# Moving the row-major loads of a decoder trunk and padding a small tile ahead of its MLP's activations

## The chip, the core and the metric

The kernel runs on one core of a Trainium2 chip. The metric is device time of one execution in microseconds (us). PE is TensorE (the page lists its weight loads as PEld), DVE is VectorE, ACT is ScalarE, POOL is GpSimd; SP issues most of the DMAs.

## What is computed

Two decoder layers on 256 tokens of width 2048, all in float32. Each layer is a token mixer, a cross-attention to 256 memory rows and a squared-ReLU MLP of width 8192, each behind an RMSNorm, with plain residual adds, and a final RMSNorm.

```python
for i in range(2):
    h = rms_norm(x, g_mix[i])
    x = x + (chunked_gmlp(h, ...) if i == 0 else s5_glu(h, ...))
    x = x + memory_attention(rms_norm(x, g_xattn[i]), rms_norm(mem, g_mem[i]), ...)
    x = x + square(relu(rms_norm(x, g_ff[i]) @ w_up[i])) @ w_down[i]
return rms_norm(x, g_final)
```

The gMLP computes z = gelu(h @ w_in + b_in), a LayerNorm on one half of z, a 128x128 causal mix within each of 16 heads, a product with the other half, and an output projection.

## The kernel before

**Numbers in two parts.** Every float32 operand is split into a rounded high part and a low part (`split`, L100: an ACT copy makes the high part, a DVE subtraction the low part), and a product is three matmuls: high by high, high by low, low by high. Weights come from HBM in tiles of 512 KB (`wload`, L115, on SP's queue, four `wraw` buffers) and are split into `whi` and `wlo` (three buffers each). One weight tile feeds 12 matmuls of 512 columns in the token form (`gemm_tok`, L129; `gemm_hid`, L547), where the activation is the stationary operand and the weight the moving one. In the feature form (`gemm_feat`, L151) the weight is stationary; a pair is one matmul of 512 columns (L163) and one of 256 (L165).

**Order.** The Tile framework orders each engine's instructions at compile time, from priorities in program order and its own model of when inputs are ready; each engine then runs its list strictly in order. After each weight tile `tick` (L81) runs what is due: `at(n, f)` puts f behind n more ticks, and `side` is a list of which one entry is taken per tick. `lag` lowers the priority of what `side` runs.

**The start (gmlp, L275).** `features(j)` loads a feature-major chunk of x on SP's queue and scales it into the stationary operand. `tokens(j)` loads a row-major chunk of x (512 KB, SP's queue) and has ACT sum its squares (two `junk` squares, L176). `zin(n)` multiplies by one 512-column chunk of w_in (eight weight tiles, chunks 4 to 7 first) and evicts: rstd from the sums of squares, a bias load on POOL's queue, two DVE operations (L316), and a Gelu on ACT. During the first chunk `side` holds features 1 to 3 and tokens 0 to 3; then `flush` empties it. PSUM has two `acc` buffers, so chunk n+2 needs chunk n's eviction. `mixing(q)` prepares the spatial weights (a load, a POOL mask, a split); its `wsr` tile shares two buffers with the bias tiles. `mem_stats` (L246) loads the row-major memory rows in four chunks on POOL's queue into two buffers, for sums of squares that end in a small matmul (L258); it is written behind the first output chunk, but the loads need no input and the framework puts them early.

**The MLP (mlp, L510).** Four blocks per layer: eight `gemm_feat` make 16 hidden feature groups into tiles `hh` and `hl` (four each, 4096 bytes per partition), then four `gemm_hid` (L558 to L560) multiply them, as the stationary operand, by w_down. The last of layer 1 is `gemm_last` (L579 to L581). The pool `ml` begins with `r2`, two floats, before `hh`, `hl` and `r`; a tile takes a multiple of 32 bytes. In the program built from this kernel the addresses within a partition are, modulo 512 bytes:

| tiles | stationary | moving | matmuls |
|---|---|---|---|
| token form: `act` by `whi`, `wlo` | 448 | 448 | L145 to L147 |
| feature form: `whi`, `wlo` by `act` | 448 | 448 | L163, L165 |
| MLP layer 0: `hh`, `hl` by `whi`, `wlo` | 256 | 448 | L558 to L560 |
| MLP layer 1: `hh`, `hl` by `whi`, `wlo` | 352 | 448 | L558 to L560 |

All slices of these tiles start at multiples of 512 bytes from the tile's address.

Of the kernel before, what the change touches and what calls it, by code (L numbers as in the profile page):

```python
# [9 lines left out]
F32 = mybir.dt.float32  # L10
# [6 lines left out]
P = 128  # L17
# [4 lines left out]
NCH = D // NB  # L22
# [16 lines left out]
class Trunk:  # L39
# [75 lines left out]
    def wload(self, w, n, kc):  # L115
        raw = self.wp.tile([P, KB * NB], F32, name="wraw", bufs=4)
        k, c = w.shape[3:]
        self.nc.sync.dma_start(out=raw.rearrange("p (k c) -> p k c", k=k), in_=w[n, kc])
        return raw

    def wtile(self, w, n, kc, raw=None):
# [124 lines left out]
    def mem_stats(self, pool):  # L246

        nc = self.nc
        ss = self.new_ss()
        for j in range(NCH):  # L250
            m = pool.tile([P, 2, NB], F32, name="memc")
            nc.gpsimd.dma_start(out=m, in_=self.a["mem"][j])
            self.sumsq(m, ss, j)
        self.rstd_mem = self.rstd(ss, "rstd_mem", self.const)
        self.rows_mem = self.const.tile([P, 2, P], F32, name="rows_mem")
        pt = self.ps([P, 2, P])
        for t in range(2):
            nc.tensor.matmul(pt[:, t, :], self.rstd_mem[:, t:t + 1].broadcast_to([P, P]), self.ident,  # L258
                             start=(t == 0), stop=True, skip_group_check=True)
        nc.scalar.copy(out=self.rows_mem, in_=pt)  # L260
# [14 lines left out]
    def gmlp(self, x, nxt):  # L275
        nc, a, tc = self.nc, self.a, self.tc
        with tc.tile_pool(name="gm", bufs=2, reuse_waits="tile") as gp:
# [3 lines left out]
            def features(j):  # L281
                xt = gp.tile([P, 4, S], F32, name="memc")
                for h in range(0, 4, 2):
                    nc.sync.dma_start(out=xt[:, h:h + 2], in_=a["x_t"][j][:, h:h + 2])
                    if j == 0 and h == 0:
                        first.append(self.wload(a["a_w_in"], NCH, 0))
                self.scale_chunk(xt, 0, hT, j)

            def tokens(j):
                cs = slice(j * NB, (j + 1) * NB)  # L290
                nc.sync.dma_start(out=x[:, :, cs], in_=a["x"][j])
                self.sumsq(x[:, :, cs], ss, j)

            first = []
            features(0)
            self.lag = 0
            self.side += [lambda j=j: features(j) for j in range(1, NCH)]
            self.side += [lambda j=j: tokens(j) for j in range(NCH)]
            rstd = None

            vh = gp.tile([P, KT, 2, P], F32R, name="vh", bufs=1)
# [5 lines left out]
            def zin(n, out):  # L307
                nonlocal rstd
                acc = self.gemm_tok(hT, a["a_w_in"], n, raw=first)
                if rstd is None:  # L310
                    self.flush()
                    self.lag = 100
                    rstd = self.rstd(ss, "rstd")
                b = self.bc(gp, a["a_b_in"][n * NB:(n + 1) * NB])
                for t in range(2):
                    nc.vector.scalar_tensor_tensor(out=out[:, t, :], in0=acc[:, t, :], scalar=rstd[:, t:t + 1],  # L316
                                                   in1=b, op0=ALU.mult, op1=ALU.add)
                nc.scalar.activation(out=out, in_=out, func=AF.Gelu)

            def mixing(q):  # L320
                if q == 0:
                    nc.gpsimd.dma_start(out=bs, in_=a["b_s"])
                wr = gp.tile([P, 4, P], F32, name="wsr", tag="bc", bufs=2)
                nc.gpsimd.dma_start(out=wr, in_=a["w_s"][:, 4 * q:4 * q + 4, :])
                nc.gpsimd.affine_select(out=wr, in_=wr, pattern=[[0, 4], [1, P]], compare_op=ALU.is_ge,
                                        fill=0.0, base=0, channel_multiplier=-1)
                self.split(wsh[:, 4 * q:4 * q + 4, :], wsl[:, 4 * q:4 * q + 4, :], wr)

            v = self.act.tile([P, 2, NCH, NB], F32, name="v", tag="act")
            st = gp.tile([P, 2, NCH, 6], F32, name="st", bufs=1)  # L330
            for j in range(NCH):
                vc = v[:, :, j, :]
                zin(NCH + j, vc)
                if j == 1:
                    self.side += [lambda q=q: mixing(q) for q in range(4)]
                for t in range(2):
                    nc.vector.bn_stats(out=st[:, t, j, :], in_=vc[:, t, :])
            mv = gp.tile([P, 2, 2], F32, name="mv", bufs=1)
            for t in range(2):
                nc.vector.bn_aggr(out=mv[:, t, :], in_=st[:, t].rearrange("p a b -> p (a b)"))  # L340
# [49 lines left out]
            for j in range(NCH):  # L390
                if j == 3:
                    self.every = 1
                zin(j, us[j])
                if j:
                    self.at(1, lambda j=j: gate(j - 1, us[j - 1]))
                    self.at(3, lambda j=j: turn(j - 1, us[j - 1]))
# [6 lines left out]
            for j in range(NCH):  # L403
                if j == 0:
                    acc = self.gemm_tok(usT, a["a_w_out"], 0, acc=acc0, kts=range(12, KT), first=False)
                    self.mem_stats(gp)
                else:
                    acc = self.gemm_tok(usT, a["a_w_out"], j)
# [101 lines left out]
    def mlp(self, x, layer, cur, nxt):  # L510
        nc, a, tc = self.nc, self.a, self.tc
        wu, wd = a["f_w_up"][layer], a["f_w_down"][layer]
        hT = cur.act
        with tc.tile_pool(name="ml", bufs=4, reuse_waits="tile") as mp:
            r2 = mp.tile([P, 2], F32, name="r2", bufs=1)
            for b in range(DFF // D):
                hid = []
                for n in range(NCH):
                    h = mp.tile([P, 4, S], F32R, name="hh")
                    l = mp.tile([P, 4, S], F32R, name="hl")  # L520
                    for i in range(2):
                        r = mp.tile([P, 2, S], F32, name="r", bufs=2)
                        self.gemm_feat(hT, wu, 2 * (NCH * b + n) + i, r)
                        nc.vector.scalar_tensor_tensor(out=r, in0=r, scalar=0.0, in1=r, op0=ALU.max, op1=ALU.mult)  # L524
                        self.split(h[:, 2 * i:2 * i + 2], l[:, 2 * i:2 * i + 2], r)
                    hid.append((h, l))
                if b == 0:
                    rstd = cur.rstd()
                    nc.vector.tensor_tensor(out=r2, in0=rstd, in1=rstd, op=ALU.mult)
                if b == DFF // D - 1:  # L530
                    nxt.start()
                for n in range(NCH):
                    if nxt.closing and b == DFF // D - 1 and n == NCH - 1:
                        self.gemm_last(hid, wd, n, b * KT, lambda t, acc: (
                            nc.vector.scalar_tensor_tensor(  # L535
                                out=x[:, t, n * NB:], in0=acc, scalar=r2[:, t:t + 1],
                                in1=x[:, t, n * NB:], op0=ALU.mult, op1=ALU.add), nxt.finish(x, t)))
                        break
                    acc = self.gemm_hid(hid, wd, n, b * KT)
                    for t in range(2):  # L540
                        xc = x[:, t, n * NB:(n + 1) * NB]
                        nc.vector.scalar_tensor_tensor(out=xc, in0=acc[:, t, :], scalar=r2[:, t:t + 1], in1=xc,  # L542
                                                       op0=ALU.mult, op1=ALU.add)
                    if b == DFF // D - 1:
                        self.at(1, lambda n=n: nxt.chunk(x, n))
# [647 lines left out]
```

## Time and profile before

| | us |
|---|---|
| three runs: median (lowest, highest) | 2884.1 (2883.07, 2889.95) |
| the profiled execution: own time | 2886.18 |
| its span in the trace | 2884.4 |
| PE busy in the span | 2837.0 |
| DVE, ACT busy | 1831.7, 1332.5 |

The span is the time from the first to the last instruction that the profiler recorded; some 1.8 us of the execution lie outside it. Matmuls overlap, so PE counts as busy whenever one is in flight; how fast they follow each other is seen in their start times. A few per cent of matmul records can be missing.

### The profile page before, as it was taken

The numbers are of one execution on the slowest core, as the hardware profiler recorded it, in microseconds if no ns is written. First come the engines' busy times: TensorE is split into PE (matmuls) and PEld (weight loads), VectorE is DVE, ScalarE is ACT, GpSimd is POOL, SyncE is SP. The second block draws the span as 40 slices with busy tenths as digits, with TensorE's granted clock in tenths as the row PEclk, the third lists the DMA queues.
The fourth block names the chain that finished last, engine by engine and source line by source line (L and its number), as shares of the span: only waits on it lengthen the run. The fifth ranks groups of instructions, "written<-read, shape, count | busy, mean of one in ns | idle before, by whom it ended". The sixth has DMA issues, their size and how long they took to land.

```text
span 2884.4 us, 39580 instructions
## 1 busy us (share of the span) xinstructions
PE 2837.0 (98%) x15238; PEld 2365.6 (82%) x15238; DVE 1831.7 (64%) x2548; ACT 1332.5 (46%) x1714; POOL 205.4 (7%) x384
## 2 busy tenths in 40 slices
PE   8999999999999999999989999999999999999998
PEld 6778888888878888788867788888888888888886
DVE  5665655575778878787567566555556555465555
ACT  5445544444534444444455445444454344343443
POOL 1000000000022222222011000000000000000000
PEclk9999999999999999999999999999999999999999
DMA  8656655558677777777689766655566566666665
GB/s 276 216 187 192 195 176 175 176 175 232 193 215 212 224 218 222 214 219 207 214 243 281 224 201 210 184 175 183 173 185 190 188 186 188 187 192 185 188 188 148
DMA packets 180461, 579.55 MB, mean 201 GB/s; under 512 B 37440, under 2 KB 39664, under 8 KB 179504
## 3 DMA queue, kind: packets, MB, share of 16 engines
q1 hardware_dynamic: 140864, 509.67, 57.3%
q0 software_dynamic: 39264, 67.29, 8.6%
q8 instruction: 119, 1.95, 0.3%
q14 instruction: 70, 0.57, 0.1%
q10 hardware_dynamic: 144, 0.07, 0.0%
HBM read 553.88 MB, written 22.94 MB: 200 GB/s over the span
## 4 chain that ended last, share of the span: by engine, by line
PE 90%; DMA 4%; DVE 3%; issue 2%; ACT 1%; POOL 0%; SPq 0%; DVEq 0%; ACTq 0%; POOLq 0%
PE acc L163 24%; PE acc L165 12%; PE acc L560 8%; PE acc L559 8%; PE acc L558 8%; PE acc L146 8%; PE acc L147 8%; PE acc L145 8%; DVE wlo L102 1%; DMA wraw<-in_b_w_in 1%; PE ps L494 1%; PE ps L438 1%; PE ps L214 1%; DMA memc<-in_mem 1%; DMA wraw<-in_f_w_up 0%
## 5 line engine op out<-in xcount | busy, mean ns | idle before, releaser
L102 DVE TENSOR_TENSOR wlo<-wraw,whi 128x1024 fp32r<-128x1024 f32 x952 | 1164.4, 1224 | 859.6 <-ACT whi L101 857.2
L101 ACT CAST whi<-wraw 128x1024 fp32r<-128x1024 f32 x952 | 999.5, 1051 | 1314.1 <-PE acc L163 394.0
L163 PE MATMUL acc<-act,whi 128*128 128x512 f32 x3072 | 1080.4, 395 | 0.6 <-ACT whi L101 0.6
L165 PE MATMUL acc<-act,wlo 128*128 128x256 f32 x3072 | 866.1, 282 | 1.7 <-DVE wlo L102 1.6
L163 PEld LDWEIGHTS acc<-act,whi 128*128 128x128 f32 x3072 | 576.1, 188 | 130.6 <-issue 1.6
L165 PEld LDWEIGHTS acc<-act,wlo 128*128 128x128 f32 x3072 | 581.5, 189 | 6.6 <-DVE wlo L102 2.9
L145 PE MATMUL acc<-whi,act 128*128 128x512 f32 x1248 | 493.8, 396 | 13.2 <-ACT whi L101 11.8
L146 PE MATMUL acc<-wlo,act 128*128 128x512 f32 x1248 | 493.1, 395 | 10.5 <-DVE wlo L102 10.4
L147 PE MATMUL acc<-whi,act 128*128 128x512 f32 x1248 | 490.8, 393 | 0.3 <-DVE act L102 0.3
L560 PE MATMUL acc<-whi,hl 128*128 128x512 f32 x992 | 395.3, 399 | 0.0
L558 PE MATMUL acc<-whi,hh 128*128 128x512 f32 x992 | 394.8, 398 | 0.0
L559 PE MATMUL acc<-wlo,hh 128*128 128x512 f32 x992 | 393.9, 397 | 0.0
L145 PEld LDWEIGHTS acc<-whi,act 128*128 128x128 f32 x1248 | 236.6, 190 | 65.3 <-ACT whi L101 14.3
L146 PEld LDWEIGHTS acc<-wlo,act 128*128 128x128 f32 x1248 | 236.6, 190 | 63.9 <-DVE wlo L102 16.9
L147 PEld LDWEIGHTS acc<-whi,act 128*128 128x128 f32 x1248 | 236.6, 190 | 48.5 <-DVE act L102 0.7
L559 PEld LDWEIGHTS acc<-wlo,hh 128*128 128x128 f32 x992 | 186.5, 188 | 46.4 <-issue 1.0
L560 PEld LDWEIGHTS acc<-whi,hl 128*128 128x128 f32 x992 | 186.5, 188 | 46.1 <-issue 1.6
L558 PEld LDWEIGHTS acc<-whi,hh 128*128 128x128 f32 x992 | 186.5, 188 | 44.7 <-issue 0.4
L809 POOL DMA_DIRECT2D Kd<-kd x128 | 72.4, 580 | 186.4 <-issue 174.2
L542 DVE SCALAR_TENSOR_TENSOR x<-acc,r,x 128x512 f32<-128x512 f32 x62 | 43.7, 746 | 10.6 <-PE acc L560 10.5
L176 ACT ACTIVATE junk<-x 128x512 f32<-128x512 f32 x56 | 35.3, 630 | 26.2 <-DVE x L535 14.0
L101 ACT CAST hh<-r 128x512 fp32r<-128x512 f32 x64 | 39.4, 615 | 16.6 <-DVE r L524 16.3
(288 smaller groups left out, 1663.2 us busy)
## 6 DMA issues: line engine op xcount, KB each, us to landing
wraw<-in_f_w_up SPq DMA_DIRECT2D x256, 512.0 KB, 3.7
wraw<-in_f_w_down SPq DMA_DIRECT2D x256, 512.0 KB, 3.7
wraw<-in_a_w_in SPq DMA_DIRECT2D x64, 512.0 KB, 4.4
wraw<-in_x_w_q SPq DMA_DIRECT2D x64, 512.0 KB, 3.7
wraw<-in_x_w_k SPq DMA_DIRECT2D x64, 512.0 KB, 3.6
wraw<-in_x_w_v SPq DMA_DIRECT2D x64, 512.0 KB, 3.7
wraw<-in_x_w_o SPq DMA_DIRECT2D x64, 512.0 KB, 3.7
wraw<-in_b_w_out SPq DMA_DIRECT2D x64, 512.0 KB, 4.4
```

Source lines behind the costliest of these rows:

```text
L101: self.nc.scalar.copy(out=hi, in_=src)
L102: self.nc.vector.tensor_tensor(out=lo, in0=src, in1=hi.bitcast(F32), op=ALU.subtract)
L145: nc.tensor.matmul(out[t], ah[:, kt, sl], hi[:, kk, :], start=st, stop=False)
L146: nc.tensor.matmul(out[t], ah[:, kt, sl], lo[:, kk, :], start=False, stop=False)
L147: nc.tensor.matmul(out[t], al[:, kt, sl], hi[:, kk, :], start=False, stop=en)
L163: nc.tensor.matmul(acc[:, f, :], hi[:, kk, sl], both[:, kt].rearrange("p a s -> p (a s)"), start=st, stop=False, skip_group_check=True)
L165: nc.tensor.matmul(acc[:, f, 0:S], lo[:, kk, sl], ah[:, kt, :], start=False, stop=en, skip_group_check=True)
L542: nc.vector.scalar_tensor_tensor(out=xc, in0=acc[:, t, :], scalar=r2[:, t:t + 1], in1=xc, op0=ALU.mult, op1=ALU.add)
L558: nc.tensor.matmul(acc[:, t, :], ah[:, kt % 4, sl], hi[:, kk, :], start=st, stop=False)
L559: nc.tensor.matmul(acc[:, t, :], ah[:, kt % 4, sl], lo[:, kk, :], start=False, stop=False)
L560: nc.tensor.matmul(acc[:, t, :], al[:, kt % 4, sl], hi[:, kk, :], start=False, stop=en)
L809: nc.gpsimd.dma_start(out=self.Kd[q // 2][:, :, q % 2, t], in_=kd[32 * t:32 * t + 16])
```

## The change

Three things. Row-major x is no longer loaded by `side` in the first weight chunk: `tokens(0..3)` are due 1, 3, 4 and 6 ticks into the second chunk, each DMA queued on SP behind the last weight load traced by then, and the first chunk's eviction (with its Gelu and its bn_stats, which move into it) is due at tick 7 of the second chunk. Each memory-row load is queued behind the POOL instruction traced before it. And `r2` takes 56 floats in layer 0 and 32 in layer 1, so `hh`, `hl` and `r` lie 192 and 96 bytes further on: both then stand at 448 modulo 512.

```diff
     def wload(self, w, n, kc):
-        self.nc.sync.dma_start(out=raw.rearrange("p (k c) -> p k c", k=k), in_=w[n, kc])
+        self.fed = self.nc.sync.dma_start(out=raw.rearrange("p (k c) -> p k c", k=k), in_=w[n, kc]).ins
...
     def mem_stats(self, pool):
-            nc.gpsimd.dma_start(out=m, in_=self.a["mem"][j])
+            self.tc.keep_in_program_order(nc.gpsimd.dma_start(out=m, in_=self.a["mem"][j]))
...
             def tokens(j):
                 cs = slice(j * NB, (j + 1) * NB)
-                nc.sync.dma_start(out=x[:, :, cs], in_=a["x"][j])
+                with tc.issue_after(self.fed):
+                    nc.sync.dma_start(out=x[:, :, cs], in_=a["x"][j])
                 self.sumsq(x[:, :, cs], ss, j)
...
-            self.side += [lambda j=j: tokens(j) for j in range(NCH)]
...
                 if rstd is None:
                     self.flush()
                     self.lag = 100
+                    for k in range(NCH):
+                        self.at((1, 3, 4, 6)[k], lambda k=k: tokens(k))
+                    self.at(7, lambda: activate(n, out, acc))
+                else:
+                    activate(n, out, acc)
+
+            def activate(n, out, acc):
+                nonlocal rstd
+                if rstd is None:
                     rstd = self.rstd(ss, "rstd")
...
                 nc.scalar.activation(out=out, in_=out, func=AF.Gelu)
+                if n >= NCH:
+                    for t in range(2):
+                        nc.vector.bn_stats(out=st[:, t, n - NCH, :], in_=out[:, t, :])
...
-                for t in range(2):
-                    nc.vector.bn_stats(out=st[:, t, j, :], in_=vc[:, t, :])
...
         with tc.tile_pool(name="ml", bufs=4, reuse_waits="tile") as mp:
-            r2 = mp.tile([P, 2], F32, name="r2", bufs=1)
+            r2 = mp.tile([P, 32 if layer else 56], F32, name="r2", bufs=1)[:, 0:2]
```

## Rows read from the trace of the kernel before

**Rows 1.** Page, part 1: busy us, share of the span, instructions.

```profile
PE 2837.0 (98%) x15238; PEld 2365.6 (82%) x15238; DVE 1831.7 (64%) x2548; ACT 1332.5 (46%) x1714; POOL 205.4 (7%) x384
```

**Rows 2.** Windows: stretch, length, busy us (instructions) by engine, granted clock, DMA share, GB/s.

```profile
20.00:30.00 10.00, 6.35 (x22) 4.64 (x21) 1.51 (x2) 4.50 (x10) 0.53 (x1) 0.87 1.01 384
...
65.00:80.00 15.00, 12.30 (x45) 9.17 (x44) 9.09 (x11) 6.67 (x8) 2.24 (x4) 0.89 0.68 209
136.00:160.00 24.00, 20.64 (x81) 15.64 (x80) 16.08 (x20) 9.06 (x11) 2.24 (x5) 0.93 0.56 179
```

**Rows 3.** Timeline, token form, layer 0: start us, length us, instruction; 24 steps between.

```profile
100.06 0.39 PE L146 MATMUL acc<-wlo,act 128*128 128x512 f32 x1
...
105.50 0.39 PE L146 MATMUL acc<-wlo,act 128*128 128x512 f32 x1
```

**Rows 4.** Timeline, MLP layer 0 (18 steps) and layer 1 (27 steps), `gemm_hid`.

```profile
799.62 0.39 PE L560 MATMUL acc<-whi,hl 128*128 128x512 f32 x1
...
803.82 0.39 PE L560 MATMUL acc<-whi,hl 128*128 128x512 f32 x1
...
2250.09 0.39 PE L558 MATMUL acc<-whi,hh 128*128 128x512 f32 x1
...
2256.39 0.39 PE L558 MATMUL acc<-whi,hh 128*128 128x512 f32 x1
```

**Rows 5.** Page, part 5: line, shapes, xcount, busy us, mean ns.

```profile
L560 PE MATMUL acc<-whi,hl 128*128 128x512 f32 x992 | 395.3, 399 | 0.0
```

**Rows 6.** Timeline, `gemm_feat` in MLP layer 1, blocks 1 (14 pairs) and 2 (15 pairs).

```profile
2339.72 0.40 PE L163 MATMUL acc<-act,whi 128*128 128x512 f32 x1
...
2344.67 0.40 PE L163 MATMUL acc<-act,whi 128*128 128x512 f32 x1
...
2519.66 0.39 PE L163 MATMUL acc<-act,whi 128*128 128x512 f32 x1
...
2524.86 0.39 PE L163 MATMUL acc<-act,whi 128*128 128x512 f32 x1
```

**Rows 7.** Timeline of PE, gMLP start: end of tile 3, start of tiles 4 and 8.

```profile
21.94 0.39 PE L147 MATMUL acc<-whi,act 128*128 128x512 f32 x1
25.22 0.50 PE L145 MATMUL acc<-whi,act 128*128 128x512 f32 x1 [2.89 <-ACT whi L101]
...
39.87 0.39 PE L145 MATMUL acc<-whi,act 128*128 128x512 f32 x1
```

**Rows 8.** Timeline of SP's queue: DMA issues (x_t, x, weights).

```profile
14.86 0.80 SPq L284 DMA_DIRECT2D memc<-in_x_t  x2
15.71 0.65 SPq L291 DMA_DIRECT2D x<-in_x  x1
16.40 0.59 SPq L118 DMA_DIRECT2D wraw<-in_a_w_in  x1
```

**Rows 9.** Timeline of ACT, with the idle time before each and what ended it.

```profile
17.79 1.71 ACT L232 ACTIVATE act<-memc,gcol 128x256 fp32r<-128x256 f32 x4 [0.42 <-DMA memc<-in_x_t]
22.75 0.63 ACT L176 ACTIVATE junk<-x 128x512 f32<-128x512 f32 x1 [3.25 <-DMA x<-in_x]
...
24.13 1.03 ACT L101 CAST whi<-wraw 128x1024 fp32r<-128x1024 f32 x1
...
47.85 0.63 ACT L176 ACTIVATE junk<-memc 128x512 f32<-128x512 f32 x1 [2.04 <-DMA memc<-in_mem]
...
63.69 0.62 ACT L101 CAST wsh<-wsr 128x512 fp32r<-128x512 f32 x1 [4.25 <-POOL wsr L325]
...
182.64 1.05 ACT L101 CAST whi<-wraw 128x1024 fp32r<-128x1024 f32 x1 [1.67 <-PE acc L147]
```

**Rows 10.** Timelines of POOL and PE: first memory load, and L258.

```profile
17.86 0.53 POOL L252 DMA_DIRECT2D memc<-in_mem  x1 [14.41 <-DMA memc<-in_x_t]
...
235.78 0.61 PE L258 MATMUL ps<-ident,rstd_mem 128*128 128x128 f32 x4
```

**Rows 11.** Timeline of POOL behind MLP layer 0.

```profile
1445.99 0.64 POOL L844 DMA_DIRECT2D dq<-Kd  x1 [75.54 <-DVE x L542]
```

## The prediction

> **What bounds the kernel now.** I read the page's first part, then windows over the span, then PE's timeline where the change touches something. PE is busy 98% of the span [rows 1], so two things can shorten the run: the stretches in which PE stands still, and the pace at which matmuls follow each other where it doesn't. The busy share hides the second, since a matmul that follows late still overlaps its neighbour; the pace is read from start times.
>
> Standing still is rare and sits early. With one 512-column matmul every 0.227 us (below), the windows from 65 to 80 and from 136 to 160 hold 45 and 81 matmuls, worth 10.2 and 18.4 us: 4.8 and 5.6 us lost [rows 2]. Before that, tile 8 starts at 39.87 although four tiles of 12 matmuls take 10.9 us and tile 4 should have started right behind the matmul at 21.94 [rows 7]. In the window from 20 to 30 the DMA engines are full (share 1.01, 384 GB/s) while PE does half its work and the granted clock averages 0.87 [rows 2]: the stall there is one of loads.
>
> The pace differs by stage. In the token form 24 steps take 5.44 us: 226.7 ns each [rows 3]. In `gemm_hid` 18 steps of layer 0 take 4.20 us and 27 of layer 1 take 6.30 us: 233.3 ns in both [rows 4]. Shape, types and granted clock are the same, both stages run without a stall, and both move the same `whi` and `wlo`; what differs is the stationary tile. `gemm_feat` has two paces within one layer: 14 pairs in 4.95 us (353.6 ns) in block 1, 15 in 5.20 us (346.7 ns) in block 2 [rows 6].
>
> **The padding.** It adds no instruction. It moves `hh` and `hl` from 256 (layer 0) and 352 (layer 1) to 448 modulo 512 bytes, the residue of `act`, `whi` and `wlo`. The only pairing that the trace shows at the long step is the one with unequal residues, and it is long at both; the pairing at 448 with 448 is short. I take it that the step follows the residues, so that `gemm_hid` comes to the token form's 226.7 ns. Nothing else in that stage would then bind: its tiles are as large as the token form's, and that form already takes one per 12 x 226.7 ns with the same casts. Count: 992 of each of three lines [rows 5] and 96 in `gemm_last` make 3072; times 6.67 ns it is **20.5 us**. Bounds: 0 if the residue isn't the cause; a loss as large if 448 were worse than 256 and 352.
>
> The long pairs of `gemm_feat` can't be explained by their own operands, which stand at 448 everywhere; they appear only behind a `gemm_hid` block, in blocks 1 and 3 of layer 1 but not in blocks 0 and 2. I read this as a phase that a stretch at the long step leaves behind. With `gemm_hid` at the short step they should go: 2 blocks x 256 pairs x 6.9 ns = **3.5 us** in layer 1 (0 if the phase has another origin). In layer 0 small matmuls of the state-space preparation come between, and stretches of both paces alternate; between 0 and 1024 x 6.9 ns = 7.1 us I take **2.0**, near the short end, where most of its pairs lie.
>
> As layer 0's MLP gets some 12 us shorter, the preparation on POOL has less cover: its row behind that MLP shows 75.5 us of idle time that ends with the MLP's last eviction [rows 11], so POOL stays ahead.
>
> [...]
>
> **The row-major loads.** Before, SP issues x's first chunk at 15.71 and weight tile 4 only behind it at 16.40 [rows 8]; ACT then waits 3.25 us for x until 22.75, its two squares come first, and tile 4's cast starts at 24.13 [rows 9], so PE stops from 21.94 to 25.22 [rows 7]. The other x chunks and two memory-row loads (the first at 17.86 [rows 10]) do the same to tiles 5 to 7.
>
> After, tile 4's load follows x_t's directly. x_t's last half megabyte, issued at 14.86, is used at 17.79 [rows 8, 9]. The 512 KB behind it take 1.4 us more at 384 GB/s [rows 2], so tile 4 is there by about 19.5, when ACT ends the scaling begun at 17.79 (its 1.71 us); cast 1.03, PE at about 20.6, before tile 3 is done. So tile 4 starts at 21.94 + 0.23 = 22.2 and, at 2.72 us a tile, tile 8 at 33.1 instead of 39.87: **6.8 us**. The four x loads now stand on SP behind tiles 8, 10, 11 and 13, with weight loads queued behind each; 2 MB spread over a chunk of 21.8 us add 96 GB/s to the 193 GB/s of the weights, under the 384 seen.
>
> Covers. The eviction of the first chunk waits for x's sums; PSUM has two buffers, so the third chunk needs it by 22.2 + 12 x 2.72 = 54.8. Tile 13's load, which paces the last x chunk, is issued when tile 6 ends on PE (its `wraw` buffer is tile 9's, whose cast needs tile 6's `whi`), near 31 to 33; with the 7.0 us that the first x chunk took (15.71 to 22.75), 1.5 us of squares and some 4 of rstd, the eviction is done by 46. Cover 9 us. Memory rows: behind the last bias load on POOL; L258 isn't needed before 235.78 [rows 10], and PE would be 7 us earlier. In order on ACT, a square that waits for its row holds back the weight casts; the longest such wait before was 2.04 us [rows 9], and ACT idles 1.67 us per tile in that stretch [rows 9]. I charge nothing; bound 2.7.
>
> The stalls at 65 to 80 and 136 to 160 come from other chains. ACT waits 4.25 us for POOL's mask on `wsr` [rows 9], whose buffer the first eviction frees. The eviction keeps about its absolute time while PE is 6.8 us further on, so this chain may cost more or less than before: bounds plus and minus 4.8 [rows 2], taken at 0. The bn_stats move within DVE's list and change nothing.
>
> **Sum.** 20.5 + 3.5 + 2.0 + 6.8 = 32.8 us. The profiled execution took 2886.18 of its own (span 2884.4 and 1.8 around it): 2853.4. The median of the runs is 2.1 lower, so 2851.3.
>
> **Rivals.**
> (a) The start is given back. ACT, DVE and POOL run lists fixed at compile time: if the first eviction, or the Gelu behind a late bias (POOL's two shared buffers, then the wait for `wsr`), stands ahead of weight casts, ACT stops while PE drains its tiles. It decides once the eviction comes later than 54.8, or such waits exceed the lead that PE has. For it: a single wait of 4.25 us already exists [rows 9]. Price: the 6.8 us. 2884.1 - 26.0 = 2858.1.
> (b) The padding changes no step, since something other than the address (separate `hh` and `hl` tiles) makes `gemm_hid` slow. [...] Against: equal steps in two layers with other side work, and no other difference in operands. 2884.1 - 6.8 = 2877.3, with the stalls' bounds 2872 to 2885.
> (c) Slower: residue 448 for the stationary tile is worse beside the running ACT and DVE writes of this stage, so that each step of `gemm_hid` grows by the same 6.67 ns. It decides as soon as the step passes 235.5 ns (3072 x 2.2 ns eat the start's gain). 2884.1 + 20.5 - 6.8 = 2897.8. Against: `act` stands at 448 and is short.
>
> **Chances.** Forecast 0.65, (a) 0.20, (b) 0.11, (c) 0.04. The range takes the forecast and (a): at the fast end 32.8 + 4.8 for the early stalls, 2846.5, and half of the 5.1 us that layer 0's pairs could give beyond the 2.0, so 2844; at the slow end the 20.5 alone, 2863.6, so 2864. It leaves out (b) and (c) and the tails, 2 in 10. A measurement of this kernel can tell 0.3% (8.7 us) from no change: faster 0.65 + 0.20 + 0.03 of (b) = 0.88, same 0.08, slower 0.04.
>
> **What would show it.** Start to start in `gemm_hid` 226.7 ns in both layers (right), 233.3 (b), above 235 (c). Pairs of `gemm_feat` in layer 1 at 346.7 in all four blocks; if blocks 1 and 3 stay long, my phase is wrong and 3.5 us are missing. Tile 4 right behind tile 3 near 22 and tile 8 near 33, with no ACT wait for x ahead of tile 4's cast. A stop of PE near 55 at the third chunk's start, or larger losses around 60 to 80, would be (a). ACT waits for memory rows after 165 with PE idle would show the bound of 2.7 in use.

## The result and the profile after

The changed kernel takes 2869.94 us (median; 2868.25 to 2870.24) beside 2883.59 us of the kernel before on the same chip: 13.7 us gained where 32.8 were forecast. The recorded ratio, which is not the quotient of these two medians (0.9953), is 0.9943 with an interval of [0.9931, 0.9956]. The kernel is faster, by about 0.5%, but slower than the range of 2844 to 2864 allowed. The profiled span went from 2884.4 to 2868.5 us, 15.9 less.

Where it went, from the start times of PE in the two traces (us; "feat" and "hid" are the stretches of `gemm_feat` and `gemm_hid`):

| stage | before | after | difference | forecast |
|---|---|---|---|---|
| gMLP, from the span's start | 304.2 | 305.6 | +1.4 | -6.8 |
| MLP layer 0, hid (4 blocks) | 376.0 | 367.5 | -8.5 | -10.25 |
| MLP layer 0, feat (4 blocks) | 379.8 | 382.7 | +2.9 | -2.0 |
| MLP layer 1, hid | 358.2 | 348.1 | -10.1 | -10.25 |
| MLP layer 1, feat | 359.3 | 360.9 | +1.6 | -3.5 |
| everything else | 1106.9 | 1103.7 | -3.2 | 0 |

Only the two hid rows did about what they should. Most of the -3.2 in the last row is not the change's doing: from the end of layer 0's MLP to the next `gemm_feat` this trace takes 324.3 us, the one before 326.4, and the traces of the experiments below, which leave that stretch alone, 324.9 to 328.1. The rows of the trace after that answer to those before follow; `gemm_hid` now has its three matmuls in L568 to L570.

Windows of the changed kernel (stretch, length, busy us and instructions by engine, granted clock, DMA share, GB/s), for [rows 2], and two stretches more, 30 to 65 and 160 to 200:

```profile
20.00:30.00 10.00, 8.62 (x38) 6.58 (x37) 5.38 (x6) 4.24 (x5) 0.00 (x0) 1.00 0.83 302
30.00:65.00 35.00, 35.00 (x156) 28.89 (x154) 21.23 (x35) 20.07 (x32) 3.21 (x6) 1.00 0.79 259
65.00:80.00 15.00, 13.22 (x56) 10.16 (x55) 9.43 (x11) 7.79 (x9) 2.78 (x5) 1.00 0.75 248
...
136.00:160.00 24.00, 19.63 (x83) 15.32 (x82) 16.22 (x20) 9.78 (x12) 2.74 (x6) 0.93 0.60 187
160.00:200.00 40.00, 35.92 (x163) 28.92 (x162) 22.21 (x40) 19.16 (x32) 1.53 (x3) 0.96 0.69 217
```

From 20 to 30 PE does 38 matmuls where it did 22, and 56 where it did 45 from 65 to 80. New is the last line: 163 matmuls from 160 to 200. The kernel before has 198 there, and PE is busy for all of the 40 us:

```profile
160.00:200.00 40.00, 40.00 (x198) 33.73 (x197) 25.48 (x32) 18.86 (x21) 0.97 (x2) 1.00 0.64 206
```

Timeline of PE in the changed kernel: `gemm_hid` in layer 0 (18 steps), in layer 1 (27 steps), for [rows 4]; pairs of `gemm_feat` in blocks 1 and 2 of layer 1 (20 pairs each), for [rows 6]:

```profile
798.78 0.39 PE L570 MATMUL acc<-whi,hl 128*128 128x512 f32 x1
...
802.86 0.39 PE L570 MATMUL acc<-whi,hl 128*128 128x512 f32 x1
...
2249.95 0.39 PE L568 MATMUL acc<-whi,hh 128*128 128x512 f32 x1
...
2256.07 0.39 PE L568 MATMUL acc<-whi,hh 128*128 128x512 f32 x1
...
2338.92 0.40 PE L163 MATMUL acc<-act,whi 128*128 128x512 f32 x1
...
2345.99 0.40 PE L163 MATMUL acc<-act,whi 128*128 128x512 f32 x1
...
2518.90 0.40 PE L163 MATMUL acc<-act,whi 128*128 128x512 f32 x1
...
2525.96 0.40 PE L163 MATMUL acc<-act,whi 128*128 128x512 f32 x1
```

4.08 us for 18 steps and 6.12 for 27: 226.7 ns in both layers, the token form's pace [rows 3]. But 7.07 and 7.06 us for 20 pairs: 353 ns in both blocks. Block 2, short before, is long now.

Timelines of the start in the changed kernel, PE, SP's queue and ACT, for [rows 7 to 9]:

```profile
22.16 0.39 PE L147 MATMUL acc<-whi,act 128*128 128x512 f32 x1
23.17 0.50 PE L145 MATMUL acc<-whi,act 128*128 128x512 f32 x1 [0.62 <-ACT whi L101]
...
35.20 0.39 PE L145 MATMUL acc<-whi,act 128*128 128x512 f32 x1
```

```profile
15.06 0.80 SPq L284 DMA_DIRECT2D memc<-in_x_t  x2
15.91 8.81 SPq L118 DMA_DIRECT2D wraw<-in_a_w_in  x5
24.78 0.65 SPq L292 DMA_DIRECT2D x<-in_x  x1
```

```profile
18.09 1.71 ACT L232 ACTIVATE act<-memc,gcol 128x256 fp32r<-128x256 f32 x4 [0.52 <-DMA memc<-in_x_t]
22.07 1.04 ACT L101 CAST whi<-wraw 128x1024 fp32r<-128x1024 f32 x1 [2.27 <-DMA wraw<-in_a_w_in]
```

Tile 4 starts at 23.17 (before 25.22). Counted matmul by matmul, the row at 39.87 in [rows 7] is not the first of tile 8 but the tenth of tile 7; tile 8 starts three matmuls later:

```profile
40.55 0.39 PE L145 MATMUL acc<-whi,act 128*128 128x512 f32 x1
```

So tile 8 went from 40.55 to 35.20: 5.35 us gained. They are gone by 200 us, and the timelines of POOL, ACT and PE between 159 and 183 show where:

```profile
158.87 0.54 POOL L111 DMA_DIRECT2D bc<-in_a_b_in  x1 [3.66 <-DVE u L325]
159.40 1.07 POOL L252 DMA_DIRECT2D memc<-in_mem  x2
168.44 0.53 POOL L252 DMA_DIRECT2D memc<-in_mem  x1 [7.97 <-ACT junk L176]
171.01 0.53 POOL L252 DMA_DIRECT2D memc<-in_mem  x1 [2.04 <-ACT junk L176]
```

```profile
159.58 1.03 ACT L101 CAST whi<-wraw 128x1024 fp32r<-128x1024 f32 x1
166.67 0.63 ACT L176 ACTIVATE junk<-memc 128x512 f32<-128x512 f32 x1 [6.06 <-DMA memc<-in_mem]
...
168.05 1.03 ACT L101 CAST whi<-wraw 128x1024 fp32r<-128x1024 f32 x1
...
176.75 0.63 ACT L176 ACTIVATE junk<-memc 128x512 f32<-128x512 f32 x1 [2.76 <-DMA memc<-in_mem]
...
177.38 1.03 ACT L101 CAST whi<-wraw 128x1024 fp32r<-128x1024 f32 x1
```

```profile
178.46 0.50 PE L145 MATMUL acc<-whi,act 128*128 128x512 f32 x1 [2.56 <-ACT whi L101]
179.72 0.79 PE L146 MATMUL acc<-wlo,act 128*128 128x512 f32 x1 [0.76 <-DVE wlo L102]
180.31 0.63 PE L147 MATMUL acc<-whi,act 128*128 128x512 f32 x1
180.74 0.63 PE L145 MATMUL acc<-whi,act 128*128 128x512 f32 x1
```

The first memory rows are issued at 159.40, behind the bias load that waited for an eviction. ACT's list has their squares right behind the cast at 159.58; the data is there at 166.67, so ACT stands for 6.06 us with the next weight cast behind it. Two buffers hold the rows: the third and fourth load wait for those squares, and ACT waits 2.76 us once more. PE stops for 2.56 us, and from 180.31 to 182.87 its steps take 0.43 us in place of 0.227; the granted clock averages 0.62 from 178.40 to 182.80. The same three weight tiles, 52 to 54, take 14.7 us here and 8.2 in the kernel before: 6.5 us lost, 2.6 of them in tile 54, where six steps take 0.43 us each.

### The profile page after: what moved, and what is told of

Same layout as the page of the kernel before. It is cut to its first block, busy times and chain, and to the rows that moved or that the text cites. A ratio compares the mean times of both kernels' runs of the same rounds, so it can differ in the third digit from the quotient of the medians.

```text
span 2868.5 us, 39577 instructions
## 1 busy us (share of the span) xinstructions
PE 2818.8 (98%) x15238; PEld 2362.5 (82%) x15238; DVE 1831.0 (64%) x2548; ACT 1333.9 (47%) x1714; POOL 205.6 (7%) x384
## 4 chain that ended last, share of the span: by engine, by line
PE 88%; DMA 5%; DVE 3%; issue 2%; ACT 1%; POOL 0%; SPq 0%; DVEq 0%; ACTq 0%; POOLq 0%
PE acc L163 23%; PE acc L165 12%; PE acc L146 8%; PE acc L570 8%; PE acc L147 8%; PE acc L569 8%; PE acc L145 8%; PE acc L568 8%; DVE wlo L102 1%; PE ps L504 1%; PE ps L448 1%; DMA wraw<-in_b_w_in 1%; DMA Kd<-kd 1%; PE ps L214 1%; DMA wraw<-in_a_w_in 1%
## 5 line engine op out<-in xcount | busy, mean ns | idle before, releaser
L163 PE MATMUL acc<-act,whi 128*128 128x512 f32 x3072 | 1083.0, 396 | 0.3 <-ACT whi L101 0.3
L163 PEld LDWEIGHTS acc<-act,whi 128*128 128x128 f32 x3072 | 576.1, 188 | 133.5 <-issue 1.6
L146 PE MATMUL acc<-wlo,act 128*128 128x512 f32 x1248 | 491.2, 394 | 12.4 <-DVE wlo L102 12.4
L147 PE MATMUL acc<-whi,act 128*128 128x512 f32 x1248 | 489.2, 392 | 0.3 <-DVE act L102 0.3
L569 PE MATMUL acc<-wlo,hh 128*128 128x512 f32 x992 | 389.0, 392 | 0.0
L568 PE MATMUL acc<-whi,hh 128*128 128x512 f32 x992 | 388.8, 392 | 0.0
L570 PE MATMUL acc<-whi,hl 128*128 128x512 f32 x992 | 388.6, 392 | 0.0
L146 PEld LDWEIGHTS acc<-wlo,act 128*128 128x128 f32 x1248 | 236.3, 189 | 64.8 <-DVE wlo L102 17.6
L147 PEld LDWEIGHTS acc<-whi,act 128*128 128x128 f32 x1248 | 236.2, 189 | 48.4 <-DVE act L102 0.7
L570 PEld LDWEIGHTS acc<-whi,hl 128*128 128x128 f32 x992 | 186.3, 188 | 40.3 <-issue 1.6
L569 PEld LDWEIGHTS acc<-wlo,hh 128*128 128x128 f32 x992 | 186.3, 188 | 40.2 <-issue 1.0
L568 PEld LDWEIGHTS acc<-whi,hh 128*128 128x128 f32 x992 | 186.3, 188 | 39.7 <-issue 0.4
```

Of the source, the lines that this page charges most:

```text
L146: nc.tensor.matmul(out[t], ah[:, kt, sl], lo[:, kk, :], start=False, stop=False)
L147: nc.tensor.matmul(out[t], al[:, kt, sl], hi[:, kk, :], start=False, stop=en)
L163: nc.tensor.matmul(acc[:, f, :], hi[:, kk, sl], both[:, kt].rearrange("p a s -> p (a s)"), start=st, stop=False, skip_group_check=True)
L568: nc.tensor.matmul(acc[:, t, :], ah[:, kt % 4, sl], hi[:, kk, :], start=st, stop=False)
L569: nc.tensor.matmul(acc[:, t, :], ah[:, kt % 4, sl], lo[:, kk, :], start=False, stop=False)
L570: nc.tensor.matmul(acc[:, t, :], al[:, kt % 4, sl], hi[:, kk, :], start=False, stop=en)
```

## The experiments

All kernels differ from the changed kernel or the kernel before by the edit shown. Times are medians beside runs of the kernel before on the same chip; those without an interval are one run each.

### One part at a time

**Padding alone**, on the kernel before:

```diff
-            r2 = mp.tile([P, 2], F32, name="r2", bufs=1)
+            r2 = mp.tile([P, 32 if layer else 56], F32, name="r2", bufs=1)[:, 0:2]
```

> The kernel before with the padding of r2 alone. Theory: the parts add, and the padding is the whole of what the change gives and more. From the two profiles' stages it shortened the MLPs by 5.5 us (layer 0) and 8.4 us (layer 1), so this kernel should take 13 to 16 us less than before, about 2869, with gemm_hid at 226.7 ns a step and the first 300 us as before. Rival: the padding's gain includes something that the other edits make possible, and alone it gives under 10 us.

**The change without the order of the memory rows:**

```diff
-            self.tc.keep_in_program_order(nc.gpsimd.dma_start(out=m, in_=self.a["mem"][j]))
+            nc.gpsimd.dma_start(out=m, in_=self.a["mem"][j])
```

> The changed kernel with the memory rows loaded as before (as early as POOL can). Theory: ACT's two waits for memory rows near 160 to 178 us (8.8 us in the changed kernel) are what gave the start's gain back; without them tile 57 starts some 7 to 9 us earlier and the run takes 5 to 8 us less than the changed kernel, about 2863. Rival: early memory loads take the bandwidth that tiles 4 to 7 need, as before, so what is won near 160 is lost near 20 to 40 and the time stays within 2 us of the changed kernel's 2870.

**The order of the memory rows alone**, on the kernel before (the same line, the other way round):

> The kernel before with only the memory rows moved. Theory: it gains a little at the start (two of six early loads gone: 0 to 2 us at tile 8) and loses 7 to 9 us near 160 to 180 to ACT's waits for memory rows: 5 to 9 us slower than before, 2889 to 2893. Rival: the waits in the changed kernel came from the x loads' new order and not from the memory rows' place; then this kernel is at 2884 or less.

**x and the eviction alone**: the changed kernel with both of those edits taken back.

> The kernel before with only the x loads and the first eviction moved. Theory: tile 8 starts 4 to 7 us earlier and nothing gives it back: 2877 to 2880. Rival (a) of the prediction: the later eviction makes the wsr chain and the LayerNorm chain cost more, and the run stays within 2 us of before.

Measured, beside 2885.21 us of the kernel before; the gMLP's end and the start of tile 8 are PE's, from the profiles (tile 8 before: 40.55; in the changed kernel: 35.20):

| kernel | time, us | ratio | gMLP ends | tile 8 |
|---|---|---|---|---|
| padding alone | 2868.0 | 0.9937 [0.9925, 0.9950] | 300.2 | 39.63 |
| without memory order | 2862.53 | 0.9917 [0.9903, 0.9930] | 296.4 | 33.71 |
| memory order alone | 2888.31 | 1.0010 [1.0001, 1.0019] | 307.0 | 37.57 |
| x and eviction alone | 2879.67 | 0.9979 [0.9970, 0.9988] | 294.5 | 33.93 |

The padding gives 17.2 us, x with its eviction 5.5, and together they give 22.7, the sum: these two parts don't touch. The order of the memory rows takes back 7.4 of it (2869.94 against 2862.53; 9.0 if each is first set against the kernel before that ran beside it). By itself it costs only 3.1, and its interval barely leaves out no change. There it also does something good: with the early loads gone from the start, tile 8 starts at 37.57 in place of 40.55. Once x has been moved this is worth nothing (tile 8 at 33.93 with the early loads in place), and the waits alone remain.

One profile of the gMLP is worth a few us either way: the kernel before and the padding alone have the same gMLP, and it ends at 304.2 and 300.2. The split is clear even so. The changed kernel and three of the kernels below that keep its gMLP end it between 301.8 and 305.6; the seven that have x moved, with the memory rows early or their squares ordered, between 294.5 and 297.2.

The waits are the same in both kernels with the memory order; ACT's timeline in the kernel with the memory order alone:

```profile
166.45 0.63 ACT L176 ACTIVATE junk<-memc 128x512 f32<-128x512 f32 x1 [5.92 <-DMA memc<-in_mem]
...
176.82 0.63 ACT L176 ACTIVATE junk<-memc 128x512 f32<-128x512 f32 x1 [3.03 <-DMA memc<-in_mem]
```

### Is it ACT's wait, or the transfers?

The changed kernel, loads in the program's order as they are, with their squares kept in it too, so that ACT's list has them behind the casts written earlier:

```diff
-            self.sumsq(m, ss, j)
+            for t in (0, 1):
+                junk = self.sm.tile([P, NB], F32, name="junk", bufs=1)
+                self.tc.keep_in_program_order(nc.scalar.activation(
+                    out=junk, in_=m[:, t, :], func=AF.Square, accum_out=ss[:, t, j:j + 1]))
```

> The changed kernel with the eight squares of the memory rows also kept in the program's order on ScalarE, behind the casts of the weights written before them. Theory A (the cost of the memory rows is the in-order wait of ScalarE at a square for a late load, with the next weight cast behind it): the waits at the squares for memory rows fall from 8.8 us to under 2, tiles 52 and 54 step by about 2.8 us and the time falls by 5 to 8 us to about 2862 to 2865, where the kernel without the order of the memory rows stands (2862.5). Rival B (the late transfers themselves take the bandwidth of the weight stream, or the statistics' matmul holds PE): the wait shows up elsewhere and the time stays at 2868 to 2870.

> The changed kernel with the squares of the memory rows kept in the program's order, once more, beside its neighbour with transposes: about 2861 as in its first run.

Measured: 2861.55 us, ratio 0.9926 [0.9912, 0.9940]; in the second run 2863.76, ratio 0.9928 [0.9915, 0.9942]. The gMLP ends at 296.0 and 296.1. Two windows of this kernel (the first two rows move in the first):

```profile
152.00:170.00 18.00, 18.00 (x90) 15.21 (x90) 12.04 (x15) 7.84 (x9) 1.60 (x3) 1.00 0.82 286
...
160.00:200.00 40.00, 40.00 (x192) 33.52 (x191) 22.22 (x25) 16.89 (x19) 0.00 (x0) 1.00 0.64 212
```

The first two chunks of rows are issued from 154.9 on, but their squares now run from 219.1 on without a wait. The third and fourth chunk, which need the first two's buffers, are issued at 220.9 and 223.2, and only their squares wait (ACT's timeline):

```profile
225.47 0.64 ACT L255 ACTIVATE junk<-memc 128x512 f32<-128x512 f32 x1 [0.82 <-DMA memc<-in_mem]
...
228.27 0.64 ACT L255 ACTIVATE junk<-memc 128x512 f32<-128x512 f32 x1 [0.39 <-DMA memc<-in_mem]
```

8.8 us of waiting became 1.2, and PE is busy for all 18.00 us from 152 to 170, with the first megabyte of rows on its way beside the weights at 286 GB/s, and for all 40.00 us from 160 to 200. So it was not the transfers, for the first two chunks at least, whose loads stand where they stood: a square stood in ACT's list ahead of a cast, before its data could be there. With the users ordered too, the loads' order costs nothing that these runs can tell (2861.55 and 2863.76 beside 2862.53).

### What the step of a matmul goes by

The first moves every tile by 32 bytes, so that all stand at 480 modulo 512; the other two change the padding of `r2` alone, to 24 and 96 floats, and to 72 and 40 (layers 0 and 1).

```diff
         warm = self.const.tile([P, 1], F32, name="warm")
+        self.const.tile([P, 8], F32, name="shift")
...
-            r2 = mp.tile([P, 32 if layer else 56], F32, name="r2", bufs=1)[:, 0:2]
+            r2 = mp.tile([P, 96 if layer else 24], F32, name="r2", bufs=1)[:, 0:2]
```

> The changed kernel with every SBUF tile after the first constant moved on by 32 bytes, so that the weights, the activations and the inner activations all still begin at one and the same residue modulo 512, 480 in place of 448. Theory A (the pace of a matmul goes by the distance between its stationary and its moving operand): token-form and inner matmuls stay at 226.7 ns, time as the changed kernel's, about 2869. Theory B (a residue of its own is good, 448): token-form and inner matmuls all go to about 233.3 ns, which costs some 20 us in the MLP and more in the token-form stages, above 2890.

> The changed kernel with the padding at 24 floats in layer 0 and 96 in layer 1, so that the inner activations stand 128 bytes off the weights' residue in layer 0 and 256 off in layer 1. If the distance counts modulo 128, both layers stay at 226.7 ns a matmul (time about 2869); modulo 256, layer 0 goes to about 233.3 and layer 1 stays (about 2879); modulo 512, both go to 233.3 (about 2889).

> The changed kernel with the padding at 72 floats in layer 0 and 40 in layer 1, so that the inner activations stand 64 bytes off the weights' residue in layer 0 and 32 off in layer 1. If the distance counts modulo 32 both layers stay at 226.7 ns (about 2869); modulo 64, layer 0 stays and layer 1 goes to about 233.3 (about 2879); if any distance is felt, both go to 233.3 (about 2889).

Measured: 2866.75, 2874.96 and 2886.94 us. From PE's timeline in the kernel with everything at 480 (its L147 is L146 of the others, its L569 their L568; 24 steps each):

```profile
99.98 0.39 PE L147 MATMUL acc<-wlo,act 128*128 128x512 f32 x1
...
105.42 0.39 PE L147 MATMUL acc<-wlo,act 128*128 128x512 f32 x1
...
799.12 0.39 PE L569 MATMUL acc<-whi,hh 128*128 128x512 f32 x1
...
804.56 0.39 PE L569 MATMUL acc<-whi,hh 128*128 128x512 f32 x1
```

With 128 bytes between them in layer 0 (24 steps) and 256 in layer 1 (33 steps):

```profile
799.06 0.40 PE L570 MATMUL acc<-whi,hl 128*128 128x512 f32 x1
...
804.64 0.39 PE L570 MATMUL acc<-whi,hl 128*128 128x512 f32 x1
...
2260.12 0.39 PE L568 MATMUL acc<-whi,hh 128*128 128x512 f32 x1
...
2267.60 0.39 PE L568 MATMUL acc<-whi,hh 128*128 128x512 f32 x1
```

With 64 in layer 0 (24 steps) and 32 in layer 1 (30 steps):

```profile
798.76 0.39 PE L570 MATMUL acc<-whi,hl 128*128 128x512 f32 x1
...
804.36 0.39 PE L570 MATMUL acc<-whi,hl 128*128 128x512 f32 x1
...
2259.95 0.40 PE L568 MATMUL acc<-whi,hh 128*128 128x512 f32 x1
...
2266.95 0.40 PE L568 MATMUL acc<-whi,hh 128*128 128x512 f32 x1
```

| distance, bytes | 0 (at 448) | 0 (at 480) | 256 | 128 | 64 | 32 | 192, 96 [rows 4] |
|---|---|---|---|---|---|---|---|
| step, ns | 226.7 | 226.7 | 226.7 | 232.5 | 233.3 | 233.3 | 233.3 |

Moving all tiles by 32 bytes makes no difference, moving them apart does, and 256 is as good as 0. Over whole blocks, the steps with no small matmul between them average the same (232.3 to 232.4 ns at 128, 233.3 to 233.4 at the other long distances). In the distances tried, the step is short where the stationary and the moving operand begin at the same address modulo 256 bytes, and some 6 ns longer at every other distance. Why it is so, no run here shows.

### What the pairs of `gemm_feat` go by

Behind the first weight tile of a block's first `gemm_feat`, a number of transposes of the identity that is chosen for each block; nobody reads their result.

```diff
+            if self.dose and kc == 0:
+                pt = self.ps([P, 2, S])
+                for k in range(self.dose):
+                    self.tc.keep_in_program_order(nc.tensor.transpose(pt[:, 0, 0:P], self.ident, self.ident))
+                self.dose = 0
             self.tick()
```

First on the changed kernel without the memory order:

> The changed kernel with the memory rows' loads as before, and with extra transposes of the identity (their result is not used) on TensorE behind the first weight tile of a block of feature-form matmuls: in layer 1, none in block 0, one in block 1, four in block 2, eight in block 3; in layer 0, none in block 0, two in each of blocks 1 to 3. Theory A (the 346.7 or 353.6 ns of a pair is a state that TensorE keeps and that a break in the stream of 512- and 256-column matmuls resets): the pairs of layer 1 behind the transposes go to 346.7 ns in the blocks where the break is long enough, at least in block 3, and each such block falls from 90.4 us to about 89.0; the time falls by up to 4 us against 2862.5. Rival B (the pace is set by something that lasts through the block, such as where its tiles lie or what the other engines do beside it): the three blocks stay at 353.6 ns a pair and 90.4 us plus the transposes, about 0.1 us each.

Then other numbers on that kernel, and one transpose in each block on the kernel with ordered squares, which ran beside its second run above:

> The kernel with the memory rows' loads as before, with other numbers of transposes behind the first weight tile: in layer 1 one in block 0, two in block 1, three in block 2 and five in block 3; in layer 0 one in block 0 and three in blocks 1 to 3. Theory A1 (each transpose swaps the state, an even number leaves it): block 1 stays long (90.4 us and the transposes), blocks 2 and 3 are short (about 89.2). Theory A2 (any small number resets, large ones do not): blocks 1 and 2 short. Rival B (chance): no pattern. In all of them the time is within 4 us of 2862.

> The kernel with the squares in the program's order, with one transpose of the identity behind the first weight tile of blocks 1, 2 and 3 of feature-form matmuls in both layers. Theory A (a single odd break moves TensorE out of the 353.6 ns state, as one did in the run before where four and eight did not): blocks 1, 2 and 3 of layer 1 all take about 88.9 us in place of 90.4, layer 0 gains up to 1 us a block, and the time falls by 4 to 6 us below the neighbour without transposes (to about 2856). Rival B (the one block was chance): blocks of layer 1 stay at 90.4 us or differ without a pattern, and the time is the neighbour's within 2 us.

Measured: 2863.97 and 2862.72 us for the two on the kernel without the memory order. Blocks of `gemm_feat` in layer 1, us from a block's first start to the first start of the `gemm_hid` behind it, by transposes in the block (the column 0 is the changed kernel's; block 0 has eight transposes of x of its own at the same place in every kernel):

| transposes | 0 | 1 | 2 | 3 | 4 | 5 | 8 |
|---|---|---|---|---|---|---|---|
| blocks 1 to 3 | 90.4 | 88.9 (4 of 4 blocks) | 89.0 | 90.8 | 90.9 | 91.0 | 91.3 |
| block 0 | 89.7 | 89.8 | | | | | |

One transpose in each of blocks 1 to 3: 2858.55 us, ratio 0.9908 [0.9895, 0.9922], 5.2 us below its neighbour without transposes (2863.76). The step shows itself in PE's timeline of this kernel, blocks 1 and 2 (10 pairs each; L164 is L163 of the others):

```profile
2329.71 0.40 PE L164 MATMUL acc<-act,whi 128*128 128x512 f32 x1
...
2333.18 0.40 PE L164 MATMUL acc<-act,whi 128*128 128x512 f32 x1
...
2499.79 0.39 PE L164 MATMUL acc<-act,whi 128*128 128x512 f32 x1
...
2503.26 0.39 PE L164 MATMUL acc<-act,whi 128*128 128x512 f32 x1
```

347 ns a pair where the changed kernel has 353. With three transposes, block 2 of the other kernel takes 3.54 us for 10 pairs:

```profile
2499.84 0.40 PE L164 MATMUL acc<-act,whi 128*128 128x512 f32 x1
...
2503.38 0.40 PE L164 MATMUL acc<-act,whi 128*128 128x512 f32 x1
```

So the pace of a pair lasts through a block (256 pairs, 88.9 or 90.4 us), and a break of one small matmul (in four blocks) or of two (in one) near a block's start changed it; the matmuls of a block are the same in every column of the table. Both of my first ideas of it fell: that a longer break resets more surely (eight did nothing but cost 0.9 us), and that each transpose swaps the pace (three and five should have). Two, three, four, five and eight were tried in one block of layer 1 each.

Nor is it true that a large number never helps. With the padding in place, block 0 starts at the long pace like the others: its first seven pairs take 351.4 ns on average, as those of blocks 1 to 3 do. Behind its own eight transposes of x it is at 346.7 ns from the third weight tile to the end, in every trace. So the number alone doesn't decide, and the cause stays open. In layer 0 nothing follows from the transposes: its four blocks sum to 378.7 and 381.8 us in two profiles of one kernel (ordered squares) and to 383.2 with one transpose each.

This last kernel is the best of the study: 25.5 us below the kernel before and some 11 below the changed one.

## Why the prediction was wrong, step by step

Two steps failed. The memory rows, charged at nothing, cost 7.4 us. The pairs of `gemm_feat`, counted as 5.5 us won, gave nothing.

**Padding, `gemm_hid`: right.** The step came to 226.7 ns in both layers, and the blocks got 8.5 + 10.1 = 18.6 us shorter, of 20.5. The missing 1.9 is nearly all in layer 0 (8.5 of 10.25), whose steps average 227.0 to 227.5 ns over a block among the small matmuls of the preparation there; that makes some 1 us of it, and the rest was not traced. The reason given, equal residues of the two operands, holds too, with 256 as its modulus in place of 512. Rival (b) falls: the step does depend on where `hh` and `hl` lie, 226.7 against about 233 ns with nothing changed but the distance between the two tiles.

**Padding, the pairs of `gemm_feat`: wrong in sign.** I read the long pairs [rows 6] as left behind by long steps of `gemm_hid`, and counted 3.5 + 2.0 us as won. In layer 1 it cost 1.6: with `gemm_hid` short, blocks 1, 2 and 3 are long, and with 32 bytes of distance in layer 1, which makes `gemm_hid` long again, block 2 is back at 88.8 us. Long pairs stand behind a stretch at the short step just as well: 353 ns in block 2, behind `gemm_hid` at 226.7. In layer 0 the difference (+2.9) is within what two profiles of one kernel show. Two blocks against two was too thin a pattern to put a price on, and the bound of 0 was wrong as well: the pace could get longer too. Padding alone gave 17.2 us of the 26.0 counted for it, which is 8.8 of the miss: by the profiles, 5.5 counted for the pairs, 1.6 that they cost in layer 1 and 1.9 of `gemm_hid`, about as much.

**The start: right, a little large.** Tile 8 starts 5.35 us earlier in the profile, and the time of this part by itself falls by 5.5 us, of 6.8. The working put tile 8 at 33.1 but took 39.87 as its start before; with 40.55 the forecast would have been 7.4. In the changed kernel's trace it starts at 35.20, and the 2.1 us that it is late arise in tile 4. I had its load done by 19.5, but ACT waited for it until 22.07. SP issued two more weight loads within about 1 us behind it, and the load took 6.2 us to its use, where I had added 1.4 us of bandwidth to x_t's landing. That one later kernel starts tile 8 at 33.10 is luck: in the eleven profiles with this start it lies between 33.1 and 35.2. The eviction's cover held: PE is busy for all 35.00 us of the window from 30 to 65, so rival (a) as I put it, with the eviction or a late bias ahead of the casts, did not happen.

**Memory rows: the wait was priced at nothing.** "I charge nothing; bound 2.7" took the longest earlier wait for a memory row (2.04) and ACT's idle time per tile. Both are from before, where the first row was issued at 17.86 [rows 10] and squared some 17 us later. After the change they are queued on POOL behind a bias load that itself waits for DVE, and the framework, which orders ACT's list by its own model of when data arrives, put the squares close behind. The price was then the time a 512 KB load takes, 159.40 to 166.67, less the one cast of cover; I had the 7.0 us of such a load in hand, for x [rows 8, 9], and used it there. The two buffers make it happen twice. Measured: 8.8 us of ACT's waits, 7.4 us of time. The prediction's last sign named the place, ACT waits for memory rows after 165 with PE idle, but with a price of 2.7. This is rival (a) by another door: the start's gain was given back through ACT's order. That rival (a)'s 6.8 us lies near 7.4 is chance, since it was the price of another wait.

**The stalls at 65 to 80 and 136 to 160** about cancel in these two traces. Counted on the same matmuls of the gMLP (a fixed window holds other work once PE is ahead), tiles 16 to 23 take 26.9 us before and 24.4 after, and tiles 40 to 51 take 41.1 and 44.2. The first difference is mostly one between profiles: the padding alone, with the gMLP of the kernel before, takes 24.9. The second was not traced to a cause.

Together: 8.8 (padding) + 7.4 (memory rows) + 1.3 (start) = 17.5 of the 18.6 us between the forecast of 2851.3 and the 2869.9 measured.

## What to carry to other kernels

Here a load that was made later cost 8.8 us of waits at its next user in ACT's list, and 7.4 us of time; with the users pinned too, 1.2 us of waits were left. So pin the users together with the load, or leave it early. Where one matmul loop runs slower than another of the same shape, compare the addresses of its two operands: here the step was 226.7 ns where they agreed modulo 256 bytes and 232.5 to 233.3 where they did not, and one line of padding was worth 17 us. And a pattern seen in two places of a trace is worth an experiment, not a term in a sum.

## What the hardware showed that was not expected

The step of a 512-column float32 matmul was 226.7 ns with its operands 0 or 256 bytes apart (modulo 512), and 232.5 to 233.3 ns at 32, 64, 96, 128 and 192; with both at 480 in place of 448 it stayed at 226.7. The pair of `gemm_feat`, whose operands are all at distance 0, has two paces, 347 and 353 ns. One 128-column transpose near the beginning of a block took it from the longer to the shorter for the 250 pairs or so that follow, in four blocks of four; three, four, five and eight of the same transposes, in one block each, did not, though eight transposes of x do in block 0.
